# Fewer projection tiles in a kernel's first stage, in finer groups, with modulation matmuls in fours

## The chip, the core and the metric

The kernel runs on one core of a Trainium2 chip. A core has a matrix engine (PE, TensorE; PEld is its weight load), a vector engine (DVE), a scalar engine (ACT), a GpSimd engine (POOL) and a queue for transfers (SP, SyncE), each with an instruction stream of its own. The metric is the device time of one execution in microseconds; before the change it is 3466.15 us, the median of three runs.

## The reference: what is computed

One step of a hybrid layer for two groups of tokens (512 sample tokens and 128 prompt tokens, 640 columns here, width 2048):

```python
sh1, sc1, g1, sh2, sc2, g2 = split(silu(cond) @ w_mod + b_mod, 6)   # w_mod: 2048 x 12288
proj = (x * (1 + sc1) + sh1) @ w_in                                 # low-rank | gate | r,k,v of 8 head pairs | attention
att  = latent_attention(proj[attention part])
rw   = rwkv7_scan(proj[r, k, v, low-rank, gate])                    # both directions, 16 heads = 8 pairs
x = post_norm(x, g1, concat(att, rw) @ w_out)
x = post_norm(x, g2, swiglu(x * (1 + sc2) + sh2))
```

No column of `proj` can be finished before shift and scale (`sh1`, `sc1`) of all 2048 channels are known, and these need the first third of `w_mod`, 33.5 MB (64 transfers of 512 KB).

## The kernel before, in words

Activations lie transposed: 128 channels on the partitions, 640 tokens along them. The 2048 input channels are 16 contraction tiles. Each float32 product is three passes of a rounded 32-bit format (high x high, high x low, low x high), each in two halves of 320 columns, so an output tile of `proj` costs 16 x 6 = 96 matmuls of 128x320. A weight tile is loaded (`raw`, three buffers) and split on ACT and DVE into `whi` and `wlo` (two buffers each).

**First stage.** `first_mods` (L428) goes through `GROUPS`, groups of contraction tiles, four of four. For a group it computes the shift and then the scale of its channels (`wmod_chunk`, L344). `wmod_first` (L326) loads `w_mod` in tiles `wm` of 512 KB from a ring of six buffers (`N_W`) and hands out their contraction slices one after the other. The matmul of a slice has 32 columns of weights and writes a quarter of the partitions of the accumulator `x`: slice kt goes to quarter kt mod 4. A copy to `ev` and a small matmul with a constant (`x<-cst,ev`) sum the quarters and turn them into the columns `mod`. Then the four tiles x of the group are modulated and split into the operands `xh`, `xl` (`modulate`, L376).

`first_tiles` (L468) is what uses them: for each group it adds the group's contribution to the low-rank tile (`ps0`), the gate tile (`ps1`) and `N_PART` = 7 more tiles (r, k, v of pairs 0 and 1, and r of pair 2). The first two accumulate in PSUM over all groups (`acc` in the profile). The seven have their sum in SBUF: each group and half ends in an eviction, an ACT copy for the first group (L495) and a DVE addition after (`part<-m,part`). After the last group `token_shift` and a store to DRAM finish a tile.

**After it**, `main` (L501) computes the other tiles of `proj`, each over all 16 contraction tiles at once in PSUM, and `rwkv` (L954) takes the pairs one by one: load of r, k, v (`kk`), decays (`xw`, `xa`), operands (`nk`, `pr`), gram matrices (`m<-pr,nk`), an inverse (`tc`), a chain of five steps (`sv`, `xs`, `zv`), all twice per pair. `wmods` computes the other 16 column blocks of the modulation with tiles of 1 MB, four slices handed out together. When `main` ends, `attention` is spawned; when all jobs are done, the output projection and the feed-forward part follow.

**What sets the order.** Until there PE runs in the order in which the program is written out. A planner (`Jobs`, L126) writes it: each job yields an estimate of how long its next piece has to wait (`W_HOP`, `M_HOP`, `HOP`), and of the jobs that are ready the one of lowest rank goes on: `rwkv` 0, modulation 2, attention 3, `main` 4. So `main` fills what `rwkv` leaves. PE waits where an operand is late, though other work may be ready. The other engines and SP are ordered by the framework's scheduler.

Of the kernel before, what the change touches and what calls it, by code (L numbers as in the profile page):

```python
# [54 lines left out]
N_E = 3  # L55
N_W = 6
N_RAW = 3
GROUPS = ((0, 4), (4, 4), (8, 4), (12, 4))
N_PART = 7
TURN = 0.5  # L60
W_HOP = 1.0
M_HOP = 4.9
RANK_R = 0
RANK_S = 1
# [95 lines left out]
def step_kernel(ctx: ExitStack, tc: tile.TileContext, a: dict, o: dict, upto: int = 99, npairs: int = NPAIR, dbg=None):  # L160
# [24 lines left out]
    def rtile(name, n, tag, bufs, dtype=F32):  # L185
        return rp.tile([P, n], dtype, tag=tag, name=nm(name), bufs=bufs)

    def slot(name, dtype=F32):
        return rtile(name, NT, "s", N_S, dtype)
# [13 lines left out]
    def acc():  # L203
        return acc_ps.tile([P, 2, 512], F32, tag="acc", name=nm("acc"))
# [104 lines left out]
    def tiles(srcs, n, g0=0):  # L309
        return (src[g0 + g] for src in srcs for g in range(n))  # L310
# [15 lines left out]
    def wmod_first(n, c0, w):  # L326

        m = 1024 // w
        for k in range(0, KT, m):
            raw = rtile("wm", 2 * NT, "w", N_W)[:, :1024].rearrange("p (k c) -> p k c", k=m)  # L330
            DMA.dma_start(out=raw, in_=a["w_mod"][n, k: k + m, :, c0: c0 + w].rearrange("k p c -> p k c"))
            for j in range(m):
                yield raw[:, j]
            yield W_HOP

    def wmod_ahead(n):
        for k in range(0, KT, 4):
# [84 lines left out]
    ps0, ps1 = acc(), acc()  # L422
    part = [slot("part") for _ in range(N_PART)]
    jobs = Jobs(T)
# [3 lines left out]
    def first_mods():  # L428
        for k0, nk in GROUPS:
            n, c0 = divmod(k0 * P, 512)  # L430
            for q in (n, 4 + n):
                yield from wmod_chunk(q, wmod_first(q, c0, nk * P), c0, nk * P)
            for kt in range(k0, k0 + nk):
                x, h = slot("x"), edge("h")
                DMA.dma_start(out=x, in_=a["xT"][kt])
                h1.append(modulate(x, h, hslot, 0, 1, kt))
# [31 lines left out]
    def first_tiles():  # L468
        fs = (0, *range(2, 2 + N_PART), 1)
        ws = Weights(a["w_in"][f, k0 // 4][:, k0 % 4 * P: (k0 % 4 + nk) * P] for k0, nk in GROUPS for f in fs)  # L470
        for k0, nk in GROUPS:
            last = k0 + nk == KT
            while len(h1) < k0 + nk:
                yield 1.0
            yield M_HOP
            for f in fs:
                w = ws.get()
                if f < 2:
                    for k in range(nk):
                        kt = k0 + k  # L480
                        yield from mm3((ps0, ps1)[f], w, k * P, h1[kt], kt == 0, kt == KT - 1)
                    if last:
                        (low_rank, gate_input)[f]()
                    continue
                t = part[f - 2]
                for hs in (slice(0, HN), slice(HN, NT)):
                    ps = mps()[:, :HN]
                    for k in range(nk):
                        xh, xl_ = h1[k0 + k]
                        for i, (ww, xx) in enumerate(((w[0], xh), (w[0], xl_), (w[1], xh))):  # L490
                            T.matmul(ps, ww[:, k * P: k * P + P], xx[:, hs], start=k + i == 0, stop=k == nk - 1 and i == 2)
                    if k0:
                        tt(V, t[:, hs], ps, t[:, hs], ALU.add)
                    else:
                        A.copy(t[:, hs], ps)  # L495
                    yield 0.0
                if last:
                    shifted(f, t[:, :HN], t[:, HN:], edge if f % 2 else long)
                    part[f - 2] = t = None

    def main():  # L501
        yield from first_tiles()
        fs = list(range(2 + N_PART, ATT_POS)) + list(range(26, 30)) + list(range(ATT_POS, 26)) + list(range(30, 33))
        ws = Weights(tiles([a["w_in"][f] for f in fs], 4))
# [1558 lines left out]
```

## Time and profile before

| | |
|---|---|
| median of the runs (3465.1 to 3469.4) | 3466.15 us |
| the profiled execution: span | 3458.1 us |
| PE busy | 3254.0 us, 94% |
| DVE, ACT, POOL busy | 72%, 42%, 29% |
| first matmul with a modulated operand starts | 44.10 us |
| first gram matrix of pair 0 starts | 261.94 us |
| output projection and all behind it | from 1480.86 us |

The span runs from the first to the last instruction. For the profiled execution the page gives no other time; the median lies 8.05 us above its span. PE is the engine to look at: busy 94%, and where it idles, a row of waits says for what. The stretches of the program differ, so each is read by itself.

### The profile page before, as it was taken

The numbers are of one execution on the slowest core, as the hardware profiler recorded it, in microseconds if no ns is written. First come the engines' busy times: TensorE is split into PE (matmuls) and PEld (weight loads), VectorE is DVE, ScalarE is ACT, GpSimd is POOL, SyncE is SP. The second block draws the span as 40 slices with busy tenths as digits, with TensorE's granted clock in tenths as the row PEclk, the third lists the DMA queues.
The fourth block names the chain that finished last, engine by engine and source line by source line (L and its number), as shares of the span: only waits on it lengthen the run. The fifth ranks groups of instructions, "written<-read, shape, count | busy, mean of one in ns | idle before, by whom it ended". The sixth has DMA issues, their size and how long they took to land.

```text
span 3458.1 us, 70966 instructions
## 1 busy us (share of the span) xinstructions
PE 3254.0 (94%) x27682; PEld 2972.3 (86%) x27682; DVE 2499.6 (72%) x4478; ACT 1449.3 (42%) x3031; POOL 999.1 (29%) x1034
## 2 busy tenths in 40 slices
PE   7988988999999789999979999999999999999998
PEld 4677766777887678989979999999999999999997
DVE  1356766776776666467688988888887778899677
ACT  1144443443444444445453444444444444333234
POOL 0022222222222122102174544444443332222124
PEclk9999999999999799999989999999999999999998
DMA  8754444444221211076534443444343357888643
GB/s 300 246 177 136 147 145 139 158 157 144 78 62 56 73 31 40 29 252 185 154 110 138 165 130 122 145 134 129 125 142 116 118 186 282 298 285 288 222 140 120
DMA packets 284528, 527.71 MB, mean 153 GB/s; under 512 B 30432, under 2 KB 66720, under 8 KB 284192
## 3 DMA queue, kind: packets, MB, share of 16 engines
q1 hardware_dynamic: 284192, 523.18, 46.1%
q8 instruction: 217, 3.56, 0.4%
q14 instruction: 119, 0.97, 0.1%
HBM read 428.99 MB, written 92.44 MB: 151 GB/s over the span
## 4 chain that ended last, share of the span: by engine, by line
PE 58%; DVE 6%; ACT 2%; issue 2%; DMA 1%; POOL 1%; SPq 0%; ACTq 0%; DVEq 0%; POOLq 0%
PE b L114 50%; PE acc L114 4%; PE m L114 2%; DVE z L228 1%; DVE ql L228 1%; POOL z L228 1%; PE x L114 1%; ACT z L240 0%; PE acc L118 0%; DVE smx L1165 0%; DVE pr L228 0%; ACT P L1166 0%; DVE ip L228 0%; DVE raw L228 0%; DMA raw<-in_w_down_dram 0%
## 5 line engine op out<-in xcount | busy, mean ns | idle before, releaser
L228 DVE TENSOR_TENSOR ql<-raw,qh 128x512 fp32r<-128x512 f32 (+1 forms) x1064 | 887.8, 849 | 260.4 <-ACT qh L1303 247.1
L1303 ACT CAST qh<-raw 128x512 fp32r<-128x512 f32 (+1 forms) x1064 | 633.3, 610 | 830.6 <-PE b L114 647.2
L114 PE MATMUL b<-t,qh 128*128 128x320 f32 x2816 | 622.8, 310 | 8.5 <-ACT qh L1303 7.4
L228 POOL TENSOR_TENSOR raw<-raw,raw 128x512 f32<-128x512 f32 x240 | 354.4, 1477 | 804.4 <-DVE ql L228 546.2
L114 PE MATMUL b<-op,qh 128*128 128x320 f32 x2560 | 553.2, 311 | 1.9 <-ACT qh L1303 1.1
L114 PEld LDWEIGHTS b<-t,qh 128*128 128x128 f32 x2816 | 472.6, 189 | 9.7 <-ACT qh L1303 8.1
L114 PE MATMUL b<-p,qh 128*128 128x320 f32 x2112 | 468.9, 311 | 0.0
L114 PE MATMUL b<-t,ql 128*128 128x320 f32 x1408 | 436.1, 310 | 5.6 <-DVE ql L228 5.5
L114 PEld LDWEIGHTS b<-op,qh 128*128 128x128 f32 x2560 | 425.9, 189 | 4.4 <-ACT qh L1303 2.7
L114 PE MATMUL b<-op,ql 128*128 128x320 f32 x1280 | 379.0, 311 | 5.4 <-DVE ql L228 5.3
L114 PEld LDWEIGHTS b<-p,qh 128*128 128x128 f32 x2112 | 356.0, 189 | 0.3
L114 PE MATMUL b<-p,ql 128*128 128x320 f32 x1056 | 329.0, 312 | 6.9 <-DVE ql L228 6.9
L114 PEld LDWEIGHTS b<-t,ql 128*128 128x128 f32 x1408 | 265.0, 188 | 7.8 <-DVE ql L228 7.7
L114 PEld LDWEIGHTS b<-op,ql 128*128 128x128 f32 x1280 | 236.7, 189 | 8.3 <-DVE ql L228 7.9
L114 PE MATMUL b<-mh,qh 128*128 128x320 f32 x1024 | 230.4, 314 | 6.6 <-ACT qh L1303 6.6
L114 PE MATMUL acc<-xh,whi 128*128 128x320 f32 x928 | 230.3, 330 | 3.5 <-ACT P L1166 2.5
L114 PE MATMUL acc<-xl,whi 128*128 128x320 f32 x928 | 232.9, 333 | 0.0
L114 PE MATMUL acc<-xh,wlo 128*128 128x320 f32 x928 | 231.8, 332 | 0.0
L114 PEld LDWEIGHTS b<-p,ql 128*128 128x128 f32 x1056 | 199.8, 189 | 9.6 <-DVE ql L228 9.6
L228 DVE TENSOR_TENSOR raw<-raw,raw 128x512 f32<-128x512 f32 x240 | 185.4, 780 | 12.5 <-POOL raw L228 9.4
L265 ACT CAST whi<-raw 128x512 fp32r<-128x512 f32 (+1 forms) x156 | 94.9, 609 | 226.4 <-PE acc L114 138.9
L114 PEld LDWEIGHTS b<-mh,qh 128*128 128x128 f32 x1024 | 174.5, 191 | 8.3 <-ACT qh L1303 7.8
(330 smaller groups left out, 5654.5 us busy)
## 6 DMA issues: line engine op xcount, KB each, us to landing
wm<-in_w_mod_dram SPq DMA_DIRECT2D x64, 1024.0 KB, 5.3
raw<-in_w_gate_dram SPq DMA_DIRECT2D x188, 256.0 KB, 2.7
raw<-in_w_up_dram SPq DMA_DIRECT2D x188, 256.0 KB, 2.9
op<-hd SPq DMA_DIRECT2D x136, 320.0 KB, 5.4
raw<-in_w_in_dram SPq DMA_DIRECT2D x132, 256.0 KB, 2.7
wm<-in_w_mod_dram SPq DMA_DIRECT2D x64, 512.0 KB, 6.0
raw<-in_w_out_dram SPq DMA_DIRECT2D x128, 256.0 KB, 3.0
raw<-in_w_down_dram SPq DMA_DIRECT2D x128, 256.0 KB, 5.4
```

The lines of the kernel that those rows point to most:

```text
L114: self.eng.matmul(out, lhsT, rhs, start=start, stop=stop)
L228: eng.tensor_tensor(out=out, in0=x, in1=y, op=op)
L265: A.copy(hi, r)
L1303: A.copy(hi, x)
```

## The change

`GROUPS` becomes five groups of 2, 2, 4, 4 and 4 contraction tiles. `N_PART` goes from 7 to 3: only r, k, v of pair 0 stay in the first stage, the other four tiles go to `main`. `wmod_first` holds slices back until it has four, waits once (`W_HOP` 2.4 instead of 1.0 for the planner) and hands the four out together. For the two small groups a chunk is 256 columns wide, so a `wm` tile holds four slices of 256 columns instead of two of 512; it is still 512 KB, in runs of 1 KB instead of 2 KB.

```diff
-GROUPS = ((0, 4), (4, 4), (8, 4), (12, 4))
-N_PART = 7
+GROUPS = ((0, 2), (2, 2), (4, 4), (8, 4), (12, 4))
+N_PART = 3
 TURN = 0.5
-W_HOP = 1.0
+W_HOP = 2.4
...
         m = 1024 // w
+        held = []
         for k in range(0, KT, m):
             raw = rtile("wm", 2 * NT, "w", N_W)[:, :1024].rearrange("p (k c) -> p k c", k=m)
             DMA.dma_start(out=raw, in_=a["w_mod"][n, k: k + m, :, c0: c0 + w].rearrange("k p c -> p k c"))
-            for j in range(m):
-                yield raw[:, j]
-            yield W_HOP
+            held += [raw[:, j] for j in range(m)]
+            if len(held) >= 4:
+                yield W_HOP
+                yield from held
+                held = []
```

What this does to the order shows at three places. First, PE in the first stage, where a group's scale is summed up. Before, the third group's, among products of the second (`m` is a half of one of the seven tiles, `x<-cst,ev` the sum over the quarters; names with one number belong together):

```order
L114 MATMUL m_959<-xh_677,whi_913 128x320
L114 MATMUL m_959<-xl_678,whi_913 128x320
L114 MATMUL m_959<-xh_677,wlo_914 128x320
L114 MATMUL x_973<-cst,ev_951 128x2 x4
L114 MATMUL m_979<-xh_650,whi_913 128x320
L114 MATMUL m_979<-xl_651,whi_913 128x320
L114 MATMUL m_979<-xh_650,wlo_914 128x320
```

With the change, the fourth group's: the end of the third group's last tile (`acc_155`), the scale's last matmuls (`x_794`) and its sum, then the next chunk and the first product of the fourth group (`acc_154`):

```order
L114 MATMUL acc_155<-xh_651,wlo_800 128x320 x2
L114 MATMUL x_794<-wm_869,cs 32x512 x2
L114 MATMUL x_794<-wm_871,cs 32x512 x2
L114 MATMUL x_794<-wm_883,cs 32x512 x2
L114 MATMUL x_794<-wm_885,cs 32x512 x2
L114 MATMUL x_893<-cst,ev_891 128x2 x4
L114 MATMUL x_935<-wm_936,cs 32x512 x2
L114 MATMUL x_935<-wm_938,cs 32x512 x2
L114 MATMUL acc_154<-xh_904,whi_841 128x320 x2
```

Before, products that don't need this scale stand behind its sum; now none does, and the next products use it. The `wm` matmuls stand in pairs of rows (four matmuls) instead of single rows (two).

Second, the SP queue, where small weight tiles (`raw`) begin to stand among the `wm` tiles. Before:

```order
L331 DMA wm_501<-in_w_mod_dram 128x2x512
L331 DMA wm_519<-in_w_mod_dram 128x2x512
L258 DMA raw_443<-in_w_in_dram 128x512
L331 DMA wm_543<-in_w_mod_dram 128x2x512
L258 DMA raw_485<-in_w_in_dram 128x512
L331 DMA wm_561<-in_w_mod_dram 128x2x512
```

Now:

```order
L332 DMA wm_405<-in_w_mod_dram 128x4x256
L258 DMA raw_340<-in_w_in_dram 128x256
L332 DMA wm_436<-in_w_mod_dram 128x2x512
L258 DMA raw_368<-in_w_in_dram 128x256
L438 DMA x_417<-in_xT_dram 128x640
L438 DMA x_426<-in_xT_dram 128x640
L332 DMA wm_438<-in_w_mod_dram 128x2x512
L258 DMA raw_460<-in_w_in_dram 128x256
```

The x tiles of the second group and the small weight tiles now stand among the `wm` tiles; all of them go through one queue, and a `wm` row waits for a buffer of the ring.

Third, PE where attention begins (`rms_s`). Before, it begins behind the grams of pair 6's second half, in front of that half's inverse:

```order
L114 MATMUL acc_13323<-cst,rms_s 128x128 x5
L114 MATMUL m_13410<-ks_11869,cst 128x320
L114 MATMUL m_13413<-cst,v_11752 64x64 x10
L114 MATMUL m_13428<-ks_11869,cst 128x320
L114 MATMUL acc_13431<-cst,rms_s 128x128 x5
L114 MATMUL m_13466<-cst,vr_13404 64x64 x10
```

Now it begins in the chain of pair 7's first half (`xs`, `zv`, `sv`), with no product between its steps:

```order
L114 MATMUL m_14248<-xs_14243,uf_162 64x64 x4
L114 MATMUL acc_14255<-cst,rms_s 128x128 x5
L114 MATMUL m_14289<-zv_13851,bk_13852 64x64 x4
L114 MATMUL m_14298<-sv_13850,pr_13669 64x64
L114 MATMUL m_14298<-sv_13850,pr_13670 64x64
```

The scan is further ahead of the rest when attention starts: between the first `rms_s` row and the scan's last one (`m<-sg,gw` of pair 7) stand 725 PE rows before and 376 now, and between that and the output projection 342 before and 560 now.

## The prediction

> **What bounds the kernel now.** I read the table of busy time by stretch first, then PE's waits. Columns: stretch, length, busy time of PE, PEld, DVE, ACT and POOL, granted PE clock, share of the transfer engines, GB/s.
>
> ```profile
> 30.00:40.00 10.00, 8.11 (x34) 1.41 (x29) 0.69 (x1) 0.00 (x0) 0.00 (x0) 0.87 1.05 387
> 50.00:60.00 10.00, 10.00 (x66) 8.40 (x63) 2.25 (x4) 2.42 (x5) 0.00 (x0) 1.00 0.73 236
> 60.00:70.00 10.00, 10.00 (x56) 6.14 (x54) 1.39 (x2) 2.74 (x6) 0.00 (x0) 1.00 0.58 163
> 70.00:80.00 10.00, 10.00 (x56) 6.64 (x55) 1.38 (x2) 2.31 (x5) 0.00 (x0) 1.00 0.71 233
> 80.00:90.00 10.00, 10.00 (x64) 7.94 (x63) 1.55 (x3) 2.74 (x6) 0.00 (x0) 1.00 0.69 210
> 0.00:200.00 200.00, 178.80 (x984) 113.03 (x984) 64.00 (x129) 35.83 (x61) 1.99 (x13) 0.97 0.75 254
> 320.00:1110.00 790.00, 728.05 (x9405) 587.51 (x9400) 545.58 (x1217) 347.07 (x894) 190.05 (x316) 0.96 0.38 124
> ```
>
> Until 44 us transfers bound the kernel (share 1.0, 387 GB/s). From 50 us PE is busy without a gap and the transfers are throttled to some 210 GB/s, because the six `wm` buffers are freed only as PE gets to them. So the first stage is PE's after its start, and PE's time there is what an edit can save. PE's waits, first 0 to 200 us, then 200 to 320 us:
>
> ```profile
> PE x L114 <- DMA wm<-in_w_mod_dram: 17.2, 14, 8.2
> ...
> PE m L114 <- DVE nk L228: 9.0, 1, 9.0
> PE m L114 <- DVE tc L601: 6.3, 1, 6.3
> PE m L114 <- ACT kk L240: 5.7, 1, 5.7
> ```
>
> **Fours instead of twos.** The groups of PE work from 0 to 215 us and from 0 to 1486 us, and single rows of the timeline (start, length, operation):
>
> ```profile
> L114 PE MATMUL x<-wm,cs 128*32 128x512 f32 x288 | 72.0, 648 | 20.0 <-DMA wm<-in_w_mod_dram 19.3 <-DVE mod L237 0.3 <-DVE mod L228 0.3
> L114 PE MATMUL x<-wm,cs 128*32 128x512 f32 x768 | 137.6, 630 | 20.8 <-DMA wm<-in_w_mod_dram 20.1 <-DVE mod L237 0.3 <-DVE mod L228 0.3
> 52.88 0.31 PE L114 MATMUL m<-xh,wlo 128*128 128x320 f32 x1
> 53.11 1.05 PE L114 MATMUL x<-wm,cs 128*32 128x512 f32 x4
> ...
> 54.35 0.31 PE L114 MATMUL m<-xl,whi 128*128 128x320 f32 x1
> 54.49 0.31 PE L114 MATMUL m<-xh,wlo 128*128 128x320 f32 x1
> 185.75 0.31 PE L114 MATMUL m<-xh,wlo 128*128 128x320 f32 x1
> 185.99 1.07 PE L114 MATMUL x<-wm,cs 128*32 128x512 f32 x8
> ...
> 187.23 0.31 PE L114 MATMUL m<-xl,whi 128*128 128x320 f32 x1
> ```
>
> A float32 matmul leaves two records: x4 is two matmuls, x8 four. Two take 1.05 us and four 1.07, since each of the four writes another quarter. Products follow each other every 0.147 us (54.35 to 54.49 us), so what one insertion pushes back is 54.35 - 52.88 - 2 x 0.147 = 1.18 us for two, and 187.23 - 185.75 - 0.29 = 1.19 for four. The first stage has 128 such matmuls in 64 twos. Afterwards it has 24 fours of 512 columns and 16 of 256 columns; a narrow four lies between half of 1.07 and all of it; I take half (all would be 9 us more of PE, in the transfers' shadow of the first two groups, so 0). 64 x 1.05 = 67 becomes 24 x 1.07 + 16 x 0.54 = 34 us: PE is spared 33 us. The new `W_HOP` is only the planner's number and costs nothing by itself.
>
> **What stands against it: less to do beside the transfers.** Four of nine tiles leave the stage: 4 x 96 x 0.147 = 56.4 us of PE work are only moved behind it (the evictions that go with them run on DVE and ACT beside PE, which is the busy one there). With 34 us of modulation and 5 x 14.1 us of products the stage is no longer full, so I follow it by its transfers. The path from a scale's last `wm` matmul to the first product:
>
> ```profile
> 37.69 1.05 PE L114 MATMUL x<-wm,cs 128*32 128x512 f32 x4 [0.30 <-DMA wm<-in_w_mod_dram]
> 38.79 0.69 DVE L356 COPY ev<-x 128x512 f32<-128x512 f32 x1 [11.97 <-PE x L114]
> 44.10 0.56 PE L114 MATMUL acc<-xh,whi 128*128 128x320 f32 x2
> ```
>
> 6.4 us. In the SP queue 1.2 MB land by 8.2 us (PE's first wait, 8.2 us). Up to the third group's last `wm` tile the new queue holds 24.9 MB (32 `wm`, 13 x, 13 weight tiles, one `wm` of 1 MB for later, the constants): at 387 GB/s 8.2 + 23.7 / 0.387 = 69 us. Groups 1 and 2 (8.8 us of products each) are done by then, in the transfers' shadow, with PE idle between. Products of group 3 start at 69 + 6.4 = 76 us. A full group then has 4 x 5 x 6 x 0.147 = 17.6 us of products, 8 fours of 1.18 and two sums of 1.1, 29 us, and since the scale's sum stands behind the last product, most of 6.4 us more: 33.5 us. Its transfers, 10.7 MB, need 27.6 us and hide. Group 4 starts at 109.5, group 5 at 143. After its gaps PE starts at half speed; the price is seen behind the wait for `nk`:
>
> ```profile
> 261.94 2.90 PE L114 MATMUL m<-pr,nk 64*128 64x128 f32 x16 [8.99 <-DVE nk L228]
> 266.00 0.73 PE L114 MATMUL acc<-xl,whi 128*128 128x320 f32 x2
> 266.53 0.73 PE L114 MATMUL acc<-xh,wlo 128*128 128x320 f32 x2
> 268.20 1.16 PE L114 MATMUL m<-pr,nk 64*128 64x128 f32 x16
> 274.00 0.46 PE L114 MATMUL acc<-xl,whi 128*128 128x320 f32 x2
> 274.29 0.46 PE L114 MATMUL acc<-xh,wlo 128*128 128x320 f32 x2
> 231.80 2.29 PE L114 MATMUL m<-cst,kk 128*128 128x2 f32 x10 [5.71 <-ACT kk L240]
> ```
>
> Pairs every 0.53 instead of 0.29 us and grams of 2.90 instead of 1.16 for 6 us: about 3 us lost. Once on the path (group 3): group 5 starts at 146. Its products and three fours take 21 us, six products of the next tile 1, then the wait for `kk`, which I leave at 6: its path (shift, store, load, square) is the same. From `kk` to the first gram before: 261.94 - 231.80 = 30.1 us, set by DVE; unchanged. First gram at 146 + 21 + 1 + 6 + 30 = 204 instead of 262 us. At that point PE has done 862 products before and 556 now, and two fours less: 306 x 0.147 + 2.4 = 47 us to come. Equal work stands at 251 against 262: **the first stage gives 10 us**, not 33, since the missing tiles leave PE idle.
>
> What is uncertain is the 1 KB runs of the first two groups (9.7 MB, 25 us at 387 GB/s). Transfers alone on the queue, KB each and us to landing:
>
> ```profile
> raw<-in_w_uq_dram SPq DMA_DIRECT2D x12, 256.0 KB, 2.6
> raw<-in_w_uk_dram SPq DMA_DIRECT2D x8, 128.0 KB, 2.0
> ```
>
> Runs of 2 KB and of 1 KB: half the runs' length lands 0.6 us earlier. So a run's cost falls with its length. The bounds are equal bandwidth (0 us) and equal time per run (25 us later); the row is nearer the first, and I add nothing.
>
> By the Trainium skill, page "DMA: Bandwidth & Descriptors", section "Why small descriptors are slow", each packet costs some three cycles beside one per 32 bytes. By that, 1 KB runs are 70/67 of the time, an estimate of 1 us later; no row of this profile can show it.
>
> **Later.** The scan now starts 58 us earlier, against 56 us of tiles handed to `main`, so `main` runs beside it as before, at 728/790 = 92% PE. What differs is where attention begins:
>
> ```profile
> 1130.00:1200.00 70.00, 47.38 (x514) 38.44 (x515) 50.80 (x96) 30.40 (x67) 12.60 (x17) 0.73 0.24 78
> 1200.00:1350.00 150.00, 134.79 (x1708) 116.92 (x1708) 105.00 (x244) 74.59 (x196) 39.12 (x60) 0.98 0.11 35
> 1390.00:1470.00 80.00, 76.53 (x558) 73.03 (x557) 33.81 (x69) 34.89 (x80) 13.96 (x19) 1.00 0.09 28
> 1141.87 2.50 PE L114 MATMUL acc<-cst,rms_s 128*128 128x128 f32 x10
> 1378.75 0.70 PE L114 MATMUL m<-sg,gw 128*128 128x320 f32 x2
> ```
>
> Beside the scan attention leaves 10% of PE idle, alone 4%. The shared stretch is 237 us for 725 rows; at 376 rows it is 123 us. The 114 us that go are half with `main` (8% idle), half alone: 114 x (0.10 - 0.06) = 5 us gained. Its beginning costs 22.6 us of idle PE plus a clock of 0.73 (47 x 0.27 = 13 us at most), as the scan sits in its inverse with nothing beside it. Now it falls into a chain without products between the steps, which waits too. The price lies between the same (0 gained) and nothing (35 gained); nearest is the same row, and I take 5.
>
> Sum: 10 + 5 + 5 = 20 us off the profiled 3458.1, so a span near 3438. The median stands 8.05 us above that span, and I keep the distance: **3446 us**.
>
> **Rivals.**
> *Every group starts idle and cold.* Scale sums queue on DVE behind the evictions and PE restarts at half speed four times: 3 more restarts of 3 us, and 3 blocks longer by some 4 us (10 of path instead of 6.4). 21 us: 3467, no change. For it speaks the 0.73 clock at 1130 to 1200; against it that PE was back at 1.00 from 50 us on, right after its first gaps. By the Trainium skill, "TensorE: Matmul & The Clock Gate", section "HAM oscillation", a PE that waits for a transfer at each contraction tile turns cold each time; the rows at 266 us agree for a gap of 9 us.
> *The ring throttles the transfers* (the other side). If the six buffers are freed as slowly as before from 50 us on, at the 210 GB/s of those rows, the 29 MB left of the stage's 46.3 MB of queue need 138 us, group 5 starts at 194 and not at 146, and all ends 48 us later: 3494. It makes the kernel slower by over 0.2% below about 250 GB/s (29 MB over 117 us). For it: the buffers are still freed in PE's order. Against it: only 17.6 us of products per group stand between, not 31.8.
> *Attention's beginning becomes free*: 28 us more, 3418. The order speaks against it, as unfilled chain steps stand there.
>
> **How the numbers follow.** Forecast 0.58, cold starts 0.20, ring 0.14, free beginning 0.08. 0.2% is 7 us, what a measurement can tell from no change. The forecast is faster but for its upper edge, the cold starts mostly within: faster 0.66, same 0.17, slower 0.17. The forecast's own range is 3426 to 3471 (25 us up by the 1 KB runs' other bound, 20 of the 30 us down that a cheaper beginning could still give). With the cold starts and a part of the two others: 3424 to 3480.
>
> **What would show it.** `wm` matmuls of the stage at 1.07 us per x8; 387 GB/s until about 70 us; PE idle in 58 to 76 us; first gram near 204 us; under 30 us lost where attention begins, the scan's last `sg,gw` some 100 us ahead of its old place. A first gram after 230 us makes the first stage wrong; one on time with no gain at the end puts the error behind it.

## The result and the profile after

The changed kernel takes 3438.59 us (median, 3431.53 to 3448.44) where the kernel before takes 3467.78 us (3465.1 to 3474.04): a ratio of 0.992, 95% interval 0.9901 to 0.9938. Timed once more, beside other kernels (`e5_change_again` below), it took 3446.61 us against 3464.2: 0.9948, 0.9936 to 0.996. So the change makes the kernel faster, by 18 us in one comparison and 29 in the other. The forecast of 3446 us lies 7 us from the first median and 1 us from the second; the two comparisons lie 11 us apart, and why they do stays open.

The profiled execution after has a span of 3446.7 us. Its whole time is 3448.44 us, the longest of the four, so the pair of profiles (3458.1 and 3446.7) shows 11 us of the gain. The kernel's time lies 1.7 to 2.0 us above the span in each of the four.

First the table of busy time by stretch, of the kernel after (stretch, length, busy time of PE, PEld, DVE, ACT, POOL with instructions, granted PE clock, share of the transfer engines, GB/s):

```profile
20.00:30.00 10.00, 6.03 (x35) 3.41 (x36) 3.66 (x8) 1.44 (x2) 0.00 (x0) 1.00 1.09 357
30.00:40.00 10.00, 10.00 (x72) 8.80 (x71) 2.21 (x6) 3.88 (x10) 0.00 (x0) 1.00 1.04 335
40.00:50.00 10.00, 6.25 (x56) 2.43 (x56) 4.09 (x9) 1.85 (x3) 0.00 (x0) 0.93 0.99 363
50.00:60.00 10.00, 10.00 (x62) 6.87 (x58) 3.55 (x8) 1.22 (x3) 0.00 (x0) 0.90 1.05 392
60.00:70.00 10.00, 8.18 (x50) 4.13 (x46) 2.74 (x5) 1.24 (x2) 0.00 (x0) 0.96 1.05 395
70.00:80.00 10.00, 8.95 (x40) 2.55 (x38) 4.89 (x11) 2.16 (x3) 0.00 (x0) 0.70 1.05 392
...
0.00:200.00 200.00, 160.96 (x1026) 109.92 (x1026) 76.97 (x155) 49.88 (x100) 13.42 (x36) 0.92 0.80 275
320.00:1110.00 790.00, 729.23 (x9358) 591.16 (x9359) 545.98 (x1212) 345.13 (x891) 197.86 (x328) 0.96 0.37 120
```

The transfers now bound the kernel until 80 us instead of 44: their share stays between 0.99 and 1.09, at 335 to 363 GB/s until 50 us and 392 to 395 after that. PE idles 39 us of the first 200 instead of 21. From 320 to 1110 us PE's busy time is the same: 729 us in 790, before 728.

Then PE's waits from 0 to 215 us, and the milestones in its timeline (start, length, operation, idle time before it and what ended it):

```profile
PE x L114 <- DMA wm<-in_w_mod_dram: 21.6, 14, 7.6
PE m L114 <- ACT kk L240: 9.0, 1, 9.0
PE m L114 <- DVE nk L228: 7.7, 1, 7.7
PE x L114 <- DVE ev L359: 4.1, 6, 0.8
```

```profile
109.82 0.56 PE L114 MATMUL acc<-xh,whi 128*128 128x320 f32 x2
...
142.46 0.90 PE L114 MATMUL acc<-xh,whi 128*128 128x320 f32 x2 [1.85 <-ACT xh L271]
...
177.99 2.29 PE L114 MATMUL m<-cst,kk 128*128 128x2 f32 x10 [9.04 <-ACT kk L240]
...
206.87 2.90 PE L114 MATMUL m<-pr,nk 64*128 64x128 f32 x16 [7.74 <-DVE nk L228]
...
1308.74 0.70 PE L114 MATMUL m<-sg,gw 128*128 128x320 f32 x2
...
1468.33 0.90 PE L114 MATMUL b<-mh,qh 128*128 128x320 f32 x2 [5.61 <-ACT qh L1306]
```

The fourth group starts at 109.8, the fifth at 142.5, pair 0's first gram at 206.9 instead of 261.9 us, the scan ends at 1309 instead of 1379, and the output projection (last row) starts at 1468.3 instead of 1480.9. Behind that row both kernels need the same: 3446.7 - 1468.3 = 1978 and 3458.1 - 1480.9 = 1977 us. So all that the change brings is made before it.

What it is made of, three stretches of the kernel before and then the same of the kernel after:

```profile
0.00:270.00 270.00, 232.31 (x1336) 158.41 (x1336) 103.08 (x192) 69.58 (x139) 22.67 (x56) 0.94 0.69 233
270.00:1110.00 840.00, 770.73 (x9983) 621.46 (x9980) 578.64 (x1290) 368.18 (x946) 198.56 (x330) 0.96 0.38 124
1110.00:1480.90 370.90, 319.42 (x3417) 281.06 (x3416) 220.86 (x499) 163.03 (x405) 82.38 (x120) 0.93 0.15 46
```

```profile
0.00:270.00 270.00, 214.72 (x1711) 152.97 (x1712) 120.54 (x244) 76.31 (x169) 25.06 (x57) 0.91 0.69 234
270.00:1110.00 840.00, 777.88 (x10013) 629.90 (x10012) 585.54 (x1295) 371.51 (x957) 209.47 (x350) 0.96 0.38 123
1110.00:1468.30 358.30, 319.24 (x3074) 286.35 (x3072) 199.04 (x432) 152.77 (x362) 67.37 (x99) 0.93 0.16 49
```

Idle PE by stretch is 37.7, 69.3 and 51.5 us before and 55.3, 62.1 and 39.1 after. The first stage idles 17.6 us more, the rest 19.6 less, and the sum stays: 158.4 and 156.5 us. PE's busy time holds a second loss, the work that is not done while only half the clock is granted; below it is called the time lost at half clock. Taken in pieces of 5 us (busy time x (1 - granted clock), summed), it is 57.0 us before and 61.2 after (in pieces of 1 us 59.6 and 66.2: the way of counting is worth a few us). What is left is PE's work at full clock: 1265.5 and 1250.6 us. So of the 12.6 us in this pair of profiles, 14.9 are less PE work, 1.9 less idle time, and 4.2 are given back at half clock. The experiments below are read by the same three numbers. A second profile of the changed kernel (`e5_change_again`) gives 157.6 us of idle time, 59.4 at half clock and 1250.3 of work, so they repeat within 2 us.

### The profile page after: what moved, and what is told of

It is laid out like the page before. It is cut to its first block, busy times and chain, and to the rows that moved or that the text cites. A ratio compares the mean times of both kernels' runs of the same rounds, so it can differ in the third digit from the quotient of the medians.

```text
span 3446.7 us, 71091 instructions
## 1 busy us (share of the span) xinstructions
PE 3244.2 (94%) x27746; PEld 2979.0 (86%) x27746; DVE 2500.1 (73%) x4469; ACT 1449.1 (42%) x3028; POOL 993.8 (29%) x1034
## 4 chain that ended last, share of the span: by engine, by line
PE 56%; DVE 4%; issue 2%; ACT 2%; DMA 1%; POOL 1%; SPq 0%; ACTq 0%; DVEq 0%; POOLq 0%
PE b L114 50%; PE acc L114 4%; PE m L114 1%; DVE z L228 1%; DVE ql L228 1%; POOL z L228 1%; PE x L114 1%; DMA z<-zd 0%; PE acc L118 0%; ACT z L240 0%; DVE smx L1168 0%; ACT P L1169 0%; DVE raw L228 0%; DMA raw<-in_w_out_dram 0%; DMA raw<-in_w_down_dram 0%
## 5 line engine op out<-in xcount | busy, mean ns | idle before, releaser
L114 PE MATMUL acc<-xh,whi 128*128 128x320 f32 x1056 | 270.0, 338 | 1.9 <-ACT xh L271 1.9
L114 PE MATMUL acc<-xl,whi 128*128 128x320 f32 x1056 | 265.1, 333 | 0.5 <-DVE xl L228 0.5
L114 PE MATMUL acc<-xh,wlo 128*128 128x320 f32 x1056 | 261.6, 330 | 0.0
L114 PEld LDWEIGHTS acc<-xh,whi 128*128 128x128 f32 x1056 | 180.9, 198 | 28.3 <-issue 13.1
L114 PEld LDWEIGHTS acc<-xl,whi 128*128 128x128 f32 x1056 | 181.2, 197 | 24.1 <-issue 14.0
```

The costliest lines, as they stand in the source:

```text
L114: self.eng.matmul(out, lhsT, rhs, start=start, stop=stop)
```

## The experiments

The theory going in was the prediction's: fours spare PE work, fewer tiles let the scan start earlier but leave PE idle behind the transfers. The rival was that only one of the parts works, or that the gain belongs to where attention happens to begin. Times are medians in us; kernels of one section ran on the same chip and share the runs of the kernel before. Tiles are counted with the low-rank and the gate tile: nine before, five after.

### One part alone, one part undone

Fours alone: the changed `wmod_first` and `W_HOP`, with the old groups and nine tiles.

```diff
-GROUPS = ((0, 2), (2, 2), (4, 4), (8, 4), (12, 4))
-N_PART = 3
+GROUPS = ((0, 4), (4, 4), (8, 4), (12, 4))
+N_PART = 7
```

> Only the fours (hold four slices, W_HOP 2.4); four groups of four and N_PART 7 as before. Theory A (the gain is PE time of the first stage: a four costs what a two did, and nine tiles still fill PE behind 44 us): 48 twos behind 44 us become 24 fours, 24 x 1.18 = 28 us less; first gram of pair 0 near 234 us instead of 262; time about 3440 us, as fast as the whole change or faster. Theory B (most of the gain is made later, by the scan standing further ahead when attention begins): under 12 us, above 3455 us.

Fours and halved groups, with nine tiles:

```diff
-N_PART = 3
+N_PART = 7
```

> The change without its N_PART: fours and five groups, but nine tiles in the first stage. Theory A: the 28 us of the fours, and products begin near 28 us instead of 44 with nine tiles to fill the transfers, some 12 us more: about 3428 us, 10 us below the whole change, with first gram near 222 us and no long idle of PE between 50 us and the end of the stage. Theory B: no tiles have moved behind the stage, so at most 12 us below before, above 3455 us.

The change without the fours (halved groups and five tiles, twos):

```diff
-W_HOP = 2.4
+W_HOP = 1.0
...
-            held += [raw[:, j] for j in range(m)]
-            if len(held) >= 4:
-                yield W_HOP
-                yield from held
-                held = []
+            for j in range(m):
+                yield raw[:, j]
+            yield W_HOP
```

> The change without the fours (twos, W_HOP 1.0): five groups, three of the seven tiles. Theory A: each of the three large groups has 16 twos of 1.18 us instead of 8 fours: 9.4 us longer per block, 28 us in all, some of it in the waits at the blocks' ends: first gram 20 to 28 us behind the changed kernel's 207 us, time 3458 to 3467 us. Theory B: the later gain stays, so within 8 us of the whole change, below 3447 us.

The change without the halved groups (fours and five tiles):

```diff
-GROUPS = ((0, 2), (2, 2), (4, 4), (8, 4), (12, 4))
+GROUPS = ((0, 4), (4, 4), (8, 4), (12, 4))
```

> The change without the halved first group: four groups of four, fours, three of the seven tiles. Theory A: products begin at 44 us and blocks of 33 us follow at 78, 111 and 144 us, where the changed kernel has its third to fifth group (78.6, about 110, 142.5): within 5 us of the whole change, 3434 to 3444 us, since what the halves let begin early ends in a wait for the third group's transfers. Rival C (the early start is worth its 17 us): 3450 us or more.

| | median | ratio to before (95%) | first gram | output projection |
|---|---|---|---|---|
| before | 3465.19 | | 261.9 | 1480.9 |
| fours, nine tiles | 3452.48 | 0.9959 (0.9945 to 0.9973) | 241.5 | 1474.0 |
| fours, halves, nine tiles | 3453.1 | 0.9965 (0.9953 to 0.9978) | 241.1 | 1471.6 |
| halves, five tiles (no fours) | 3455.39 | 0.9974 (0.9964 to 0.9984) | 217.7 | 1483.0 |
| fours, five tiles (no halves) | 3447.59 | 0.995 (0.9938 to 0.9963) | 206.0 | 1466.9 |

The last two columns are from the one profiled execution. For the kernel without fours that one took 3463.9 us, the longest of nine, so its 1483.0 says less than its median.

Fours alone came out between the two theories' numbers, and with halves and nine tiles on the rival's side. Without fours the kernel lies between them again, nearer to theory A in its time, though its first gram comes only 11 us behind the change's and not 20 to 28. Without halves it came out between its two numbers.

Three things follow. The halved groups bring nothing: without them all milestones stand within 2 us of the whole change (first gram 206.0 and 206.9), and with nine tiles they change 0.6 us. The fours are a half of the gain or more: without them it falls to 0.26%. Alone they bring 0.41%, and the tiles alone, in the next section, 0.16%: together 0.57%, about what fours and tiles bring at once (0.50%). And the gain in front of the scan is no guide to the end: with nine tiles and fours the first gram comes 20 us earlier, with the same work done (868 products before it, and 862 before the change), yet the output projection comes 7 us earlier.

Where those 13 us went is seen in the three numbers. In the run with fours alone PE's work at full clock before the output projection falls from 1265.5 to 1240.7 us, by 25; idle time is the same (157.4, before 158.4); but the time lost at half clock rises from 57.0 to 75.8. Its mean granted clock was 0.963 to 0.967 in all five executions, the kernel before's 0.968 to 0.972. So it isn't one bad execution; this kernel's order of instructions meets more half-clock stretches.

### The change again, the tiles alone, the number of tiles, the planner's number

The change once more, without an edit:

> The change itself once more, beside the next three kernels. Theory A (what the parts spare is full-clock work, and the half-clock windows that the order of the instructions happens to meet take part of it back): about 3440 us (3432 to 3448) at a mean granted clock of 0.970, some 5 to 10 us below the same kernel without the halved groups (3447.6 at 0.968). Theory B (that distance belonged to the chip or the hour): 3445 to 3450.

Five tiles alone, against the kernel before:

```diff
-N_PART = 7
+N_PART = 3
```

> Of the change only the tiles: five tiles in the first stage instead of nine, four groups, modulation in twos. Theory A (the halves bring nothing, so this is the run without fours again): 3455 us, 3450 to 3460. Theory B (with twos the halved groups are needed, because PE idles behind a first group of four contraction tiles): 3462 or more.

Seven tiles, against the kernel with fours alone:

```diff
-N_PART = 7
+N_PART = 5
```

> Fours, four groups, seven tiles in the first stage (between nine and five). Theory A (the clock that the order happens to meet decides): anywhere from 3440 to 3456, and span times granted clock within 3325 to 3338 as for nine and five tiles. Theory B (each tile that leaves gains its share evenly): 3450, within 2, at a clock between 0.964 and 0.968.

The planner's old number, against the kernel with fours alone:

```diff
-W_HOP = 2.4
+W_HOP = 1.0
```

> Fours alone (nine tiles, four groups) with the planner's number left at 1.0 instead of 2.4: the same instructions in another order. Theory A: span times granted clock stays near 3327, but the clock need not be the 0.9644 of the run with 2.4; if it is 0.969, the time is near 3437. Theory B (the number is only the planner's and nothing hangs on it; the low clock belongs to nine tiles with fours): 3452 within 3, clock 0.964 to 0.965.

| | median | ratio to before (95%) | mean granted clock, all executions |
|---|---|---|---|
| before | 3464.2 | | 0.9694 |
| the change again | 3446.61 | 0.9948 (0.9936 to 0.996) | 0.9684 |
| five tiles alone | 3459.1 | 0.9984 (0.9974 to 0.9994) | 0.9684 |
| fours, seven tiles | 3432.18 | 0.9902 (0.9887 to 0.9917) | 0.9672 |
| fours, nine tiles, planner's number 1.0 | 3449.82 | 0.9954 (0.9941 to 0.9967) | 0.9670 |

The change again lies where it stands without the halves (3447.59), so the 9 us between these two in the first comparison were not the halves' work, and my theory's number for it fell: the rival's held. Five tiles alone are 5 us faster (0.16%), at the upper edge of theory A's range; the interval just leaves out no change. The planner's number is worth nothing (0.9954 and 0.9959), though with 1.0 the first `kk` matmul comes at 233 instead of 209 us: once more, 24 us in front of the scan and none at the end. The clock there isn't the one of fours alone (0.9670 and 0.9644), which speaks against a fixed clock for nine tiles; the time lost at half clock was 71.7 us, idle time 152.9, work 1247.6.

The surprise is seven tiles: 14 us faster than the change. Neither theory said so. Theory A's range of 3440 to 3456 missed it, and theory B's 3450 too. The next runs ask whether it is one lucky order.

### Six, seven and eight tiles, and PE kept busy in three waits

Seven tiles once more (`N_PART` 5, fours, four groups), and the same kernel with `N_PART` 6 (eight tiles) and 4 (six tiles):

> Seven tiles, fours, four groups once more, beside the next three. Theory A (seven tiles fill the time behind the transfers without piling work up in front of the scan): ratio 0.990 to 0.992 to the kernel before, about 3432 us, 12 us or more below five tiles (0.9948 in the last set). Theory B (an accident of that chip): 0.994 to 0.996.

> Fours, four groups, eight tiles. Theory A (an optimum between five and nine, by idle time behind transfers on one side and work piled up in front of the scan on the other): 3434 to 3446, between seven (3432) and nine (3452). Theory B (seven tiles is one lucky order; each order has its own few us): 3446 to 3456, not below nine by more than its interval.

> Fours, four groups, six tiles. Theory A (an optimum between five and nine): 3432 to 3443, between seven (3432) and five (3447). Theory B (one lucky order): 3444 to 3452.

Seven tiles with PE kept busy in the three single waits of pair 0:

```diff
+    warmed = set()
+
+    def warm(key, n, ps):
+        if key not in warmed:
+            warmed.add(key)
+            for _ in range(n):
+                T.eng.matmul(ps[:, :P], ident, ident, start=True, stop=True)
+        return ps
...
-        ss = stat_cols(kk, con("blk2"), 2)
+        ss = stat_cols(kk, con("blk2"), 2, lambda: warm("kk", 24, mps()))
...
-            both = [mps(), mps()]
+            both = [warm('nk', 26, mps()), mps()]
...
-            ps = mps()
+            ps = warm('tc', 24, mps())
```

> The same kernel with PE kept busy in the three single waits of pair 0 (before the matmuls on kk, the first gram and the first tc): 24, 26 and 24 matmuls of 128x128 on constants, whose results are written over by the matmuls that follow. They take 6 to 7 us each, less than the waits of 8.2, 8.7 and 8.4 us. Theory A (after such a wait the clock is granted at half, and these half-clock windows cost time on the path): the first gram and the tc matmuls run at full clock (about 1.2 instead of 2.90 us for the first gram group), and the kernel is 4 to 9 us faster than without them. Theory B (DVE sets the path there, PE at half clock costs nothing): within 2 us.

With the results of the earlier sections, fours and four groups give this curve. The last six columns are from the profiled executions, up to the output projection: idle PE in three stretches, time lost at half clock, work at full clock, and where that projection starts.

| tiles | median | ratio (95%) | idle 0 to 250 | 250 to 600 | 600 to end | half clock | work | projection |
|---|---|---|---|---|---|---|---|---|
| nine | 3452.48 | 0.9959 (0.9945 to 0.9973) | 39.0 | 32.3 | 86.2 | 75.8 | 1240.7 | 1474.0 |
| eight | 3439.6 | 0.9929 (0.9917 to 0.9941) | 37.1 | 32.0 | 85.1 | 63.1 | 1243.3 | 1460.6 |
| seven | 3433.9 | 0.9908 (0.9895 to 0.9921) | 43.5 | 22.0 | 77.4 | 55.5 | 1246.7 | 1445.0 |
| six | 3439.28 | 0.9926 (0.9915 to 0.9938) | 44.7 | 27.8 | 79.1 | 61.2 | 1246.4 | 1459.1 |
| five | 3447.59 | 0.995 (0.9938 to 0.9963) | 52.1 | 22.2 | 79.7 | 62.5 | 1250.3 | 1466.9 |

Seven tiles repeat (0.9902 and 0.9908), and their neighbours on both sides lie between. So over the number of tiles there is an optimum, and seven is no lucky order. The idle time says part of why. First the stretches of fours with nine tiles, then with seven, then with five:

```profile
0.00:250.00 250.00, 211.01 (x1338) 157.01 (x1339) 106.24 (x195) 70.65 (x141) 23.52 (x56) 0.92 0.74 251
250.00:600.00 350.00, 317.70 (x4038) 249.69 (x4038) 234.66 (x515) 148.47 (x391) 84.70 (x144) 0.95 0.45 146
```

```profile
0.00:250.00 250.00, 206.50 (x1314) 148.72 (x1314) 114.64 (x217) 75.86 (x156) 24.34 (x51) 0.93 0.71 245
250.00:600.00 350.00, 328.05 (x4386) 257.80 (x4386) 240.33 (x535) 151.80 (x396) 83.61 (x152) 0.96 0.47 154
```

```profile
0.00:250.00 250.00, 197.91 (x1344) 134.35 (x1344) 108.90 (x206) 67.08 (x138) 19.74 (x48) 0.88 0.69 240
250.00:600.00 350.00, 327.77 (x4295) 258.31 (x4296) 240.39 (x537) 153.59 (x403) 86.69 (x152) 0.97 0.47 153
```

With five tiles PE idles 8.6 us more than with seven before 250 us, which fits transfers with too little work beside them. With nine it idles 10.3 us more between 250 and 600 us. That is what the prediction weighed, and it weighed only the ends. Of the 29 us from nine to seven in these profiles 15 are idle time and 20 time at half clock, with 6 more of work; of the 22 us from five to seven, 11 are idle time, 7 half clock and 4 work. (The profiles overstate these steps: the seven-tile one is the quickest of its four executions, and by the ratios to the kernel before the steps are 18 and 15 us. The profile of `e7_fours_seven_tiles`, a second one of the same kernel, has 143.9 us of idle time, 58.6 at half clock and 1245.3 of work, so the differences are the kernels'.) Idle time in the first 600 us is only a part of it. Of the 20 us at half clock between nine and seven, 18 lie behind 600 us (50.4 and 32.4), far from the stage that was changed, and there nine tiles also idle 8.8 us more; between five and seven, 10 us at half clock lie before 250 us (20.6 and 10.5). Why one order loses so much more at half clock than another I can count and not explain, so the optimum is measured and its cause is shown only in part.

The filled waits settle less than they were meant to. The timeline around the first gram, with seven tiles, without and with the fill (the L567 row):

```profile
216.91 2.90 PE L114 MATMUL m<-pr,nk 64*128 64x128 f32 x16 [8.71 <-DVE nk L228]
219.74 0.90 PE L114 MATMUL acc<-xh,wlo 128*128 128x320 f32 x2
220.44 0.73 PE L114 MATMUL acc<-xh,whi 128*128 128x320 f32 x2
```

```profile
208.71 5.97 PE L567 MATMUL m<-cst 128*128 128x128 f32 x52
217.59 0.46 PE L114 MATMUL m<-pr,nk 64*128 64x128 f32 x2 [2.92 <-DVE nk L228]
218.45 2.04 PE L114 MATMUL m<-pr,nk 64*128 64x128 f32 x14 [0.40 <-DVE nk L228]
220.42 0.90 PE L114 MATMUL acc<-xh,wlo 128*128 128x320 f32 x2
221.12 0.73 PE L114 MATMUL acc<-xh,whi 128*128 128x320 f32 x2
```

The wait shrank from 8.71 to 2.92 us, but the products behind it still take 0.73 instead of 0.46 us a pair: half clock. Behind the wait for `kk`, shrunk from 8.10 to 2.54 us, it is the same. Counted in stretches of 1 us, what is left of each of these two waits is followed by 6.8 us at half clock. What was expected of theory A (a first gram group of 1.2 us) didn't come, and the time is the same, 3433.25 against 3433.9. Theory B's number held, but its reason wasn't tested, since the clock didn't stay up behind these waits: the time lost at half clock is 55.6 us with the fill and 55.5 without. What a half-clock stretch on that path costs stays open.

## Why the prediction was right, and where it wasn't

The forecast was 3446 us, with 20 us taken off; measured are 18 and 29. The direction and the size came out, and most of the milestones. The size is in part luck: the pair of profiles, the only place where the steps can be followed, shows 12.6 us and not 20, as its execution before was a quick one and its execution after a slow one. By its steps:

**Two against four in a quarter.** A row of x8 takes 1.06 us after the change, as foreseen (59.14 in the second fence below is one), but the 33 us of spared PE are the term that was mis-sized. The groups of these matmuls, from 0 to 215 us:

```profile
L114 PE MATMUL x<-wm,cs 128*32 128x512 f32 x232 | 41.2, 663 | 8.2 <-DMA wm<-in_w_mod_dram 7.3 <-DVE mod L237 0.8
L114 PE MATMUL x<-wm,cs 128*32 128x256 f32 x128 | 13.8, 540 | 14.5 <-DMA wm<-in_w_mod_dram 14.3 <-DVE mod L228 0.3
```

They are 41.2 + 13.8 = 55 us, before 72.0: 17 us, and 14.9 of PE's work at full clock in all. Some 5 of the missing 16 us are the 16 narrow fours: 13.8 us, where 16 x 0.54 = 8.6 were counted. Eight of them that had waited for their tile take 1.08 us each, as much as a wide one, which is the bound that the prediction named and didn't take; the two single ones between products take 0.64. The other 10 are the wide fours: 29 of them (24 of the stage, five of later column blocks) at 1.07 us would be 31 us. Rows of both kinds, the narrow ones first:

```profile
9.57 1.08 PE L114 MATMUL x<-wm,cs 128*32 128x256 f32 x8 [0.90 <-DMA wm<-in_w_mod_dram]
32.53 0.64 PE L114 MATMUL x<-wm,cs 128*32 128x256 f32 x8
...
59.14 1.06 PE L114 MATMUL x<-wm,cs 128*32 128x512 f32 x8
...
63.86 2.03 PE L114 MATMUL x<-wm,cs 128*32 128x512 f32 x12
66.81 1.05 PE L114 MATMUL x<-wm,cs 128*32 128x512 f32 x4 [0.91 <-DMA wm<-in_w_mod_dram]
68.77 5.11 PE L114 MATMUL x<-wm,cs 128*32 128x512 f32 x16 [0.92 <-DMA wm<-in_w_mod_dram]
```

A wide four needs two tiles. Where tiles come as fast as they are used, its first two go when their tile is there (x4 at 66.81), and the next two wait for theirs: a four of that kind is two twos. That is about a half of the 10 us. The other half is half clock: over the row of 5.11 us the granted clock was 0.67, and three more rows (at 48.01, 75.99 and 145.23 us) ran in part or wholly at a half. I had counted all 24 wide fours at 1.07 us. The milestones below show no price for it, since most of it lies where the transfers set the path, and so the sum didn't suffer. It is also part of why the idle PE that I named as a sign is missing: from 58 to 76 us PE is idle for 2.9 us only.

**The first stage's path.** Third group forecast at 76, measured at 78.6; fourth 109.5 and 109.8; fifth 146 (with 3 us for the clock) and 142.5; the wait for `kk` left at 6, measured 9.0; first gram 204 and 206.9. Products done at that point are 556 and, before the change, 862, as counted. So the first stage gave 261.9 - 206.9 - 47 = 8 us, not 10. The error at the third group fits the 1 KB runs, for which I added 0 of a range from 0 to 25 us. The same stretches of the run with fours alone, which has runs of 2 KB, beside the row of 357 GB/s above:

```profile
8.00:20.00 12.00, 7.58 (x28) 0.91 (x24) 1.33 (x2) 1.24 (x2) 0.00 (x0) 1.00 1.05 396
20.00:30.00 10.00, 4.74 (x22) 1.52 (x20) 0.86 (x2) 0.00 (x0) 0.00 (x0) 0.73 1.05 392
```

357 against 392 GB/s is 9% less, with the transfer engines as busy (1.09 and 1.05); from 8 to 20 us it is 363 against 396. For the 9.7 MB of the two groups that is 2.4 us, and the third group was 2.6 late. The Trainium skill's three cycles for each packet (page "DMA: Bandwidth & Descriptors", section "Why small descriptors are slow") give an estimate of 1 us: the right sign, and half the measured loss.

**Behind the stage.** 10 us were forecast, 5 for a shorter stretch in which scan and attention share PE and 5 for attention's beginning. From 1110 us to the output projection PE idles 39.1 us instead of 51.5, and loses 17.6 instead of 16.0 at half clock: 11 us gained, of the forecast size. But it is made at one place. The 70 us in which attention begins, beside the row of 1130 to 1200 us before:

```profile
1175.00:1245.00 70.00, 56.93 (x612) 47.19 (x611) 52.65 (x108) 32.84 (x81) 15.29 (x24) 0.78 0.24 77
```

There idle time and half clock cost 25 us instead of 35, so 10 are gained at attention's beginning, where I had taken 5, and hardly any in the rest of the shared stretch, which is as short as forecast (122 us, forecast 123). And 8 us in the first stage and 11 behind 1110 us make 19, while the pair of profiles shows 12.6 at the output projection: some 6 are lost again between the first gram and 1110 us, a stretch for which I had counted nothing. There PE idles 2 us longer than before and loses 2 more at half clock; the rest is within what this way of counting can tell. The scan's end came 70 us ahead of its old place and not 100, as attention begins 45 us later (1186.7 instead of 1141.9).

**The distance of 8 us** between the median and the profiled span was kept, and was no property of the kernel. The time lies 1.7 to 2.0 us above the span; that profiled execution was one of the quick ones. Taking 20 us off the median is the same sum, so nothing hung on it.

**The rivals.** Cold starts at each group: half clock in 0 to 270 us costs 14.9 us instead of 10.7, so 4 us, not 21, and the blocks of groups 3 and 4 took 31.2 and 32.7 us, no longer than the 33.5 forecast. The ring: the transfer engines were as good as fully busy until 80 us, at 335 GB/s or more, and group 5 started at 142.5 us and not at 194, so it didn't throttle; that fell clearly. Attention's beginning for nothing: idle time there fell by 12 us, not 28.

**What no step of it saw.** First, that of three edits one, the halved groups, does nothing, which only undoing it showed. Second, that five tiles aren't the right number: seven, with the fours and without the halves, takes 3432 to 3434 us where the change takes 3447 on the same chip as the first of these; with or without the fill it is the fastest of all kernels here. Third, that the time at half clock differs by 20 us between orders of the same work. I had priced the clock at 3 us, at one place.

## What to carry to other kernels

Read idle time, half-clock time and full-clock work of the busiest engine apart, up to the point behind which two kernels are equal: an earlier milestone in front of a long stretch (20 us here) can leave nothing at its end. When work is taken from a stage that is bound by transfers, the best amount to leave can lie between the ends (here seven of nine tiles), so try those in between too. Instructions that are put together in fours save time only where their operands are there together.

## What the runs showed of the hardware that was not expected

A wait much shorter than expected can bring PE's clock down. Stretches of 1 us of the kernel after (columns as in the first table), around a single wait of 1.59 us, and the row of the timeline behind that wait:

```profile
482.21 2.04 PE L114 MATMUL m<-pr,nk 64*128 64x128 f32 x14 [1.59 <-ACT us L240]
...
481.00:482.00 1.00, 0.00 (x0) 0.00 (x0) 0.97 (x3) 0.91 (x3) 0.83 (x4) 1.00 0.68 168
482.00:483.00 1.00, 0.79 (x7) 0.82 (x9) 1.00 (x3) 0.20 (x1) 1.00 (x1) 0.57 1.06 412
483.00:484.00 1.00, 1.00 (x11) 0.96 (x8) 0.73 (x1) 0.10 (x1) 0.18 (x1) 0.50 1.04 404
...
485.00:486.00 1.00, 1.00 (x7) 1.00 (x6) 0.97 (x2) 0.62 (x2) 0.00 (x0) 0.72 0.79 262
```

The granted clock is full during the wait, halves as PE comes back to work, and stays at half for 3.4 us: 2 x (1 - 0.57) = 0.86 in the second stretch, 2 in the two whole ones, and 2 x (1 - 0.72) = 0.56 in the last. So one gap of 1.6 us costs 1.7 us of PE work on top of itself. The Trainium skill (page "TensorE: Matmul & The Clock Gate", section "HAM oscillation") gives the rule as no idle gaps above 3.4 us; here less than a half of that is enough.

Not every such gap does it. Two rows of the same kind in the same kernel, each with the stretch of 5 us in and behind it:

```profile
746.94 1.13 PE L114 MATMUL m<-pr,nk 64*128 64x128 f32 x14 [1.54 <-DVE y L228]
747.00:752.00 5.00, 5.00 (x34) 4.55 (x36) 2.07 (x3) 2.84 (x8) 0.22 (x1) 0.66 0.56 209
882.40 1.13 PE L114 MATMUL m<-pr,nk 64*128 64x128 f32 x14 [1.66 <-DVE y L228]
882.00:887.00 5.00, 4.60 (x45) 4.19 (x46) 2.33 (x5) 1.84 (x6) 0.04 (x1) 1.00 0.39 120
```

The wait of 1.54 us is followed by half clock (0.66 on average over 5 us), the longer one of 1.66 us is not. Of the eleven waits of 1.5 to 2.5 us between 206 and 1110 us seven are followed by it and four, up to 2.48 us long, are not; what decides it no run here shows. From all causes together the kernel before loses 57 us at half clock before its output projection, as much as 57 / 1.7 = 33 such stretches, and between the kernels here it is 55 to 76 us.

And transfers in runs of 1 KB move 357 GB/s where runs of 2 KB move 392, on the same queue in the same stretch (20 to 30 us) of two kernels.
